# Wide products behind the four groups of a triangular inverse, and LayerNorm statistics from transposed blocks, in an encoder layer on one core

## The chip, the cores and the metric

The kernel runs on one core of a Trainium2 chip. The metric is the device time of one execution in microseconds; the median of 3 timed runs of the kernel before is 2743.46 us (2743.14 to 2744.37). The engines are called as the profile does: PE (TensorE, the products; PEld its weight loads), DVE (VectorE), ACT (ScalarE), POOL (GpSimd) and SP, which issues the DMAs.

## The reference: one encoder layer

Two groups of 512 tokens (a prompt and a sample), 1024 features, all in float32, shared weights:

```
x = LN(alpha*x + 0.5*SwiGLU_1(x))                      # d_ff 2816
h = x @ W_in                                           # MLA, RWKV-7 and gate columns
A = MLA(h_q, h_kv) @ P_mla ; B = RWKV7_bidir(h_rwkv) @ P_rwkv
x = LN(alpha*x + (sig(g_A)*A + sig(g_B)*B) @ W_o)      # LayerNorm 2
x = LN(alpha*x + CrossAttn(x, LN(mem)))                # LayerNorm 3
x = LN(alpha*x + 0.5*SwiGLU_2(x))
```

The RWKV-7 part has 8 heads of 64 and runs over the sequence in both directions. Per step the state S becomes `S*w + (S a) b^T + v k^T`, and the output is `S r`. LayerNorm is the plain one: mean and variance over the 1024 features of each token.

## The kernel before

**Products.** A float32 operand is held as two parts, hi and lo, each rounded for TensorE (fp32r); a product of two operands is hi·hi + hi·lo + lo·hi, three TensorE instructions of 128x512 for a block of 128 of the summed dimension. In names xh, xl (mh, ml; coh, col) are the parts of activations and whl both parts of a weight tile. `split` (L243-246) makes them: ACT casts the high part (L245), and the low part, the difference, is taken on an engine that the caller picks: POOL (L246) or DVE (all DVE operations show L179, a helper).

**Weights** of the middle of the program come through `Stream` (L113-150). A slot is a tile 128x1024, eight blocks: a DMA into wraw, the cast on ACT, the low part on `self.low`, at the moment `fetch` is called. `ahead` is how many slots are fetched before they are needed, 1 during the recurrence, where `low` is POOL.

**Stages**, by the trace of before: FFN 1 to about 715 us, projection and MLA to 1209, the recurrence to about 1750, mixing of the two branches and LayerNorm 2 to 1890, cross attention and LayerNorm 3 to 2065, FFN 2 and LayerNorm 4 to the end.

**The recurrence** (`Recurrence`) handles four pairs of heads in turn, h = 0 to 3. For each pair `front` builds the chunk matrices: 32 blocks (two directions, two groups, eight chunks of 64 tokens) of products ar,bk, masked into phi. `inverse` then inverts the unit triangular 64x64 matrices of these blocks: both 32x32 diagonal halves by forward substitution, all systems at once, on DVE (`for i in range(1, 31)`: a product tm, a step into dw, an add into dw), after which two DVE transposes give xt and ct; then the off-diagonal half by small TensorE products. These come in four groups of 32 products 32x32 per e (64 records each): two groups xt,phi, whose banks are copied to qt; two groups ct,qt, whose banks are copied into phi. Eight diagonal copies phi<-ct stand between. In these lines `k.in_order` fixes the order of the products among themselves. `chunks` runs the recurrence proper over the chunks, with products of 64x64.

TensorE would be idle for much of that, so `rec.beside` is a generator of wide products (the gates, the projections of the memory, the MLA output), and `Recurrence.fill(n)` takes n steps of it, a step being the three products of one k-block. The table `FILL` gives three numbers for each pair: steps asked for in the front, in the substitution (spread evenly over its 30 steps) and in the chunks. What is left at the last pair is done in `early_rows`.

**Norms 2 and 3** (`RowNorm`, L366-391) add up x and x² while the eight row blocks of 128 features come in: ACT squares, POOL (group 0) or DVE (group 1) adds x, DVE adds the squares; eight products with a column of 1/1024 (`mean`) then give mean and mean square per token. **Norms 1 and 4** (`BlockNorm`, L394) transpose the blocks on TensorE against an identity (cc), four 128x128 transposes into one bank, and take bn_stats of the bank on DVE (ln_b), then bn_aggr. PSUM banks carry tags: a has four banks, b and c two each (`Bank`).

**Order.** Each engine runs its instructions in an order that a scheduler fixes when the program is built; it moves work forward where it believes that there is room, so an instruction need not stand where the code has it.

Of the kernel before, what the change touches and what calls it, by code (L numbers as in the profile page):

```python
# [20 lines left out]
P = 128  # L21
T = 512
G = 2
# [37 lines left out]
FILL = ((72, 66, 30), (6, 50, 36), (8, 54, 36), (0, 38, 20))  # L61
# [302 lines left out]


class RowNorm(Norm):  # L366


    def add(self, n):
        nc, y = self.k.nc, self.y(n)  # L370
        if n == 0:
            self.s1, self.s2 = self.tile("ln_s1", 2), self.tile("ln_s2", 2)
        sq = self.tile("sq", 4) if n else self.s2
        nc.scalar.activation(out=sq, in_=y, func=AF.Square)
        if n:
            eng = nc.gpsimd if self.tags[0] == "c" else nc.vector
            eng.tensor_tensor(out=self.s1, in0=self.s1 if n > 1 else self.y(0), in1=y, op=ALU.add)
            nc.vector.tensor_tensor(out=self.s2, in0=self.s2, in1=sq, op=ALU.add)

    def stats(self):  # L380
        k, nc, sb = self.k, self.k.nc, self.sb
        st = Bank(k, self.tags[0])
        for o, t in enumerate((self.s1, self.s2)):
            for b in range(4):
                st.mm(st.t[:, 4 * o + b : 4 * o + b + 1], t[:, b * P : b * P + P], k.mean)
        m = sb.tile([P, 3, 4], F32, name="ln_m", tag="ln_m", bufs=2)
        mean, var, sq = m[:, 0], m[:, 1], m[:, 2]
        nc.vector.tensor_copy(m[:, 0:2], st.t[:, 0:8].rearrange("p (a b) -> p a b", b=4))
        nc.vector.scalar_tensor_tensor(out=sq, in0=mean, scalar=-1.0, in1=mean, op0=ALU.mult, op1=ALU.mult)
        nc.vector.scalar_tensor_tensor(out=var, in0=sq, scalar=LN_EPS / ALPHA**2, in1=var, op0=ALU.add, op1=ALU.add)  # L390
        Norm.spread([self], mean, var)
# [414 lines left out]
def kernel(  # L806
# [58 lines left out]
    k.mean = cp.tile([P, 1], F32, name="mean")  # L865
    nc.vector.memset(k.mean, 1.0 / D)
# [386 lines left out]
    with pool("rw") as sb:  # L1253
# [11 lines left out]

        rec.memory = memory_norm(k, sb, mem, d_mt)
# [45 lines left out]
    def norms_of(i):  # L1312
        return [RowNorm(k, sb, lambda n, g=g: x32[g][:, n], f"ln{i}_g", f"ln{i}_b", "cb"[g] * 2) for g in range(G)]

    for q in range(4):
        for g in range(G):
            nc.sync.dma_start(out=x32[g][:, 2 * q : 2 * q + 2], in_=d_x1[g][:, 2 * q : 2 * q + 2])
# [693 lines left out]
```

## Time and profile before

| | |
|---|---|
| median of 3 runs | 2743.46 us (2743.14 to 2744.37) |
| profiled execution, its own time | 2749.23 us |
| its span | 2747.4 us |
| granted clock of TensorE, mean | 0.971 |

The profile's page gives each engine's busy share, the span in 40 slices with the granted clock, the waits and the groups of instructions. Queries of the trace cut it into windows: length, busy time of each engine and the clock granted there. A length less PE's busy time is TensorE's idle time.

### The profile page before, as it was taken

What the parts mean: (1) busy time and instruction counts of PE and PEld (TensorE: products, weight loads), DVE (VectorE), ACT (ScalarE), POOL (GpSimd) and SP (SyncE); (2) the same over time, 40 slices, a digit from 0 to 9 for tenths busy, and PEclk for the clock granted to TensorE, in tenths of its full rate; (3) what the DMA queues carried; (4) which work ended last, traced back from release to release, by engine and by line L of the source; (5) the groups of instructions that cost most, each with busy time, mean ns of one, the idle gap of its engine ahead of it and who ended that gap; (6) DMA issues with size and microseconds to landing.
All of it is one profiled execution on the core that took longest, in us unless ns stands there. A gap on an engine that the chain in (4) does not pass through costs nothing.

```text
span 2747.4 us, 41481 instructions
## 1 busy us (share of the span) xinstructions
PE 2597.5 (95%) x15600; PEld 2074.1 (75%) x15600; DVE 2118.7 (77%) x3745; ACT 1090.2 (40%) x2004; POOL 699.2 (25%) x479
## 2 busy tenths in 40 slices
PE   8999999999999999997989888999999999999996
PEld 7888887787767777776677676777777888887784
DVE  7888887999466777758475768657788888887988
ACT  5344332222453555444443433224554433342222
POOL 0233332443200001133123331103031323232443
PEclk9999999999999999998999898999999999999998
DMA  4344337671244333343434353541102433347751
GB/s 173 123 154 161 146 135 297 237 264 64 92 171 157 114 97 112 115 139 136 132 110 128 119 179 116 166 157 46 47 31 81 165 143 139 141 173 266 275 200 65
DMA packets 164200, 396.08 MB, mean 144 GB/s; under 512 B 41056, under 2 KB 47456, under 8 KB 164000
## 3 DMA queue, kind: packets, MB, share of 16 engines
q1 hardware_dynamic: 164000, 393.43, 40.9%
q8 instruction: 124, 2.03, 0.3%
q14 instruction: 76, 0.62, 0.1%
HBM read 259.41 MB, written 133.96 MB: 143 GB/s over the span
## 4 chain that ended last, share of the span: by engine, by line
PE 54%; DVE 11%; issue 3%; ACT 3%; DMA 2%; POOL 1%; SPq 0%; POOLq 0%; ACTq 0%; DVEq 0%
PE ps L215 51%; PE ps L220 3%; DVE whl L179 1%; DVE dw L179 1%; DVE x L179 1%; DVE z L179 1%; DVE rs L179 1%; DVE phi L179 1%; DVE tm L179 1%; DVE ln_s L179 1%; DMA ld<-d_rw 1%; DVE wt L179 0%; ACT whl L245 0%; DMA d_q<-st 0%; POOL ln_z L357 0%
## 5 line engine op out<-in xcount | busy, mean ns | idle before, releaser
L215 PE MATMUL ps<-xo,whl 128*128 128x512 f32 x3792 | 899.3, 396 | 14.1 <-DVE z L179 8.5
L215 PE MATMUL ps<-xh,whl 128*128 128x512 f32 x2688 | 889.3, 402 | 15.7 <-ACT xh L245 11.4
L215 PEld LDWEIGHTS ps<-xo,whl 128*128 128x128 f32 x3792 | 712.9, 189 | 185.7 <-DVE z L179 6.7
L215 PEld LDWEIGHTS ps<-xh,whl 128*128 128x128 f32 x2688 | 508.1, 190 | 132.0 <-ACT xh L245 13.0
L215 PE MATMUL ps<-xl,whl 128*128 128x512 f32 x1344 | 536.5, 399 | 1.4 <-POOL xl L246 1.4
L179 DVE TENSOR_TENSOR whl<-wraw,whl 128x512 fp32r<-128x512 f32 (+4 forms) x269 | 280.4, 1052 | 53.2 <-ACT whl L245 52.7
L245 ACT CAST whl<-wraw 128x512 fp32r<-128x512 f32 (+4 forms) x314 | 219.7, 711 | 247.2 <-PE ps L215 226.4
L215 PEld LDWEIGHTS ps<-xl,whl 128*128 128x128 f32 x1344 | 255.9, 190 | 56.4 <-POOL xl L246 2.7
L712 POOL TENSOR_TENSOR s<-s,up 128x512 f32<-128x512 f32 x80 | 116.4, 1455 | 624.0 <-DVE up L179 399.7
L245 ACT CAST whl<-wt 128x512 fp32r<-128x512 f32 (+3 forms) x280 | 148.5, 555 | 272.5 <-PE ps L215 160.7
L179 DVE TENSOR_TENSOR whl<-wt,whl 128x512 fp32r<-128x512 f32 (+3 forms) x280 | 215.5, 791 | 11.5 <-ACT whl L245 11.4
L246 POOL TENSOR_TENSOR whl<-wraw,whl 128x1024 fp32r<-128x1024 f32 x45 | 109.4, 2433 | 385.8 <-ACT whl L245 353.3
L245 ACT CAST hop<-s 128x512 fp32r<-128x512 f32 x128 | 79.5, 621 | 246.1 <-POOL s L712 180.3
L179 DVE TENSOR_TENSOR hop<-s,hop 128x512 fp32r<-128x512 f32 x128 | 121.4, 949 | 58.3 <-ACT hop L245 50.7
L179 DVE SCALAR_TENSOR_TENSOR x<-ps,x 128x512 f32<-128x512 f32 x184 | 124.5, 683 | 53.6 <-PE ps L215 53.0
L179 DVE TENSOR_TENSOR wt<-wraw 128x512 f32<-128x512 f32 (+3 forms) x140 | 109.9, 785 | 1.0
L179 DVE TENSOR_TENSOR wt<-wraw,wt 128x512 f32<-128x512 f32 (+3 forms) x140 | 102.8, 734 | 4.6 <-DMA wraw<-in_wf_dram 2.6
L610 POOL TENSOR_TENSOR x<-x,s 128x512 f32<-128x512 f32 x48 | 70.6, 1476 | 129.4 <-DVE x L179 129.4
L246 POOL TENSOR_TENSOR xl<-x,xh 128x512 fp32r<-128x512 f32 x48 | 66.8, 1420 | 98.2 <-ACT xh L245 97.9
L179 DVE TENSOR_TENSOR p<-ps,p 128x512 f32<-128x512 f32 x120 | 82.2, 685 | 7.2 <-PE ps L215 4.0
L610 POOL TENSOR_TENSOR x<-x,z 128x512 f32<-128x512 f32 x48 | 71.2, 1485 | 52.8 <-DVE x L179 49.2
L215 PE MATMUL ps<-mh,whl 128*128 128x512 f32 x256 | 81.1, 397 | 1.3 <-ACT whl L245 1.3
(328 smaller groups left out, 3715.9 us busy)
## 6 DMA issues: line engine op xcount, KB each, us to landing
d_h<-hop SPq DMA_DIRECT2D x140, 512.0 KB, 2.6
xo<-d_h SPq DMA_DIRECT2D x140, 512.0 KB, 7.2
wraw<-in_wf_dram SPq DMA_DIRECT2D x95, 512.0 KB, 3.4
wraw<-in_wa_dram SPq DMA_DIRECT2D x57, 512.0 KB, 3.5
wraw<-in_wb_dram SPq DMA_DIRECT2D x32, 512.0 KB, 3.4
wraw<-in_wf_dram SPq DMA_DIRECT2D x36, 384.0 KB, 3.7
ld<-d_rw SPq DMA_DIRECT2D x24, 512.0 KB, 4.8
d_gate<-t SPq DMA_DIRECT2D x32, 256.0 KB, 2.3
```

Source lines behind the costliest of these rows:

```text
L179: inst = f(*args, **kw)
L215: self.last = order(k.tc, k.nc.tensor.matmul(out, a, b, start=start, stop=stop), self.last)
L220: self.last = order(self.k.tc, self.k.nc.tensor.transpose(out, a, ident), self.last)
L245: nc.scalar.copy(hi, src)
L246: (low or nc.vector).tensor_tensor(out=lo, in0=src, in1=hi.bitcast(F32), op=ALU.subtract)
L610: eng.tensor_tensor(out=y[r, c], in0=y[r, c], in1=u, op=ALU.add)
L712: nc.gpsimd.tensor_tensor(out=s[:, i], in0=s[:, i], in1=up[:, i], op=ALU.mult)
```

## The change

1. `FILL` asks for fewer steps in the substitution, and a new table `BESIDE` gives the steps that are placed directly behind each of the inverse's four groups: 2, 4, 2, 3 in the first three pairs, 0, 2, 0, 1 in the last. The sum of all steps is as before, since the generator is the same.
2. All four qt copies are on DVE (before, half of them were on ACT), and DVE's diagonal copies phi<-ct are ordered behind the last of them.
3. While the loop of the substitution is being emitted, `low` of the weight stream is DVE, and POOL again after it. Of the 45 low parts of 128x1024 that POOL had, 26 stay there; DVE has 74 in place of 55. Of the 19, six belong to the first pair, five each to the second and third, three to the fourth. In DVE's order 4, 2, 3 and 1 of them stand ahead of the four substitutions' first steps; 2, 3, 2 and 2 stand inside (the fourth pair's behind its last tm).
4. LayerNorms 2 and 3 are `BlockNorm`s: no squares on ACT, no running sums, no mean products; 32 transposes, eight bn_stats and four bn_aggr per norm and group. `add` is called after row blocks 3 and 7.
5. The weights of FFN 2 are set up before `out_rows(1)`, and three of its tiles are requested within it (`fw.ahead(1)`, after row blocks 7, 11 and 15 of its steps). The pool ow is opened earlier for that.

In the program's order, counted from a pair's last ar,bk product, the steps ahead of the first xt,phi product were 43, 47.3, 43.7 and 35.3, and are 32.7, 41.3, 33.7 and 37.3.

**TensorE around the inverse of the first pair, before.** The names xt,phi and ct,qt are the small products, xh and xl with whl the fill.

```order
L215 MATMUL ps<-xl_5605,whl 128x512
L215 MATMUL ps<-xh_5604,whl 128x512
L215 MATMUL ps<-xt,phi 32x32 x64
L215 MATMUL ps<-ct,qt 32x32 x25
L215 MATMUL ps<-xh_11155,whl 128x512
L215 MATMUL ps<-ct,qt 32x32 x6
L215 MATMUL ps<-xl_11156,whl 128x512
L215 MATMUL ps<-xh_11155,whl 128x512
L215 MATMUL ps<-ct,qt 32x32 x18
L215 MATMUL ps<-xh_11155,whl 128x512
L215 MATMUL ps<-ct,qt 32x32 x12
```

**The same place in the changed kernel.**

```order
L217 MATMUL ps<-xl_5603,whl 128x512
L217 MATMUL ps<-xh_5602,whl 128x512
L217 MATMUL ps<-xt,phi 32x32 x32
L217 MATMUL ps<-xh_5602,whl 128x512
L217 MATMUL ps<-xl_5603,whl 128x512
L217 MATMUL ps<-xh_5602,whl 128x512 x2
L217 MATMUL ps<-xl_5603,whl 128x512
L217 MATMUL ps<-xh_5602,whl 128x512
L217 MATMUL ps<-xt,phi 32x32 x32
L217 MATMUL ps<-xh_5600,whl 128x512
L217 MATMUL ps<-xl_5601,whl 128x512
L217 MATMUL ps<-xh_5600,whl 128x512 x2
```

The first 64 rows of xt,phi were one run and are two of 32, with two steps between; four steps follow the second, two the first run of ct,qt and three the second.

**DVE at the end of the substitution and in the copies of the first pair, before** (tm, dw: the substitution; qt<-ps the copies out of the xt,phi banks).

```order
L179 SCALAR_TENSOR_TENSOR dw<-dw,lw 128x29
L179 TENSOR_TENSOR dw<-dw,tm 128x29
L179 SCALAR_TENSOR_TENSOR dw<-dw,lw 128x30
L179 STREAM_TRANSPOSE xt<-dw 128x32x32
L179 STREAM_TRANSPOSE ct<-dw 128x32x32
L179 COPY phi<-ct 32x16x32 x4
L179 COPY qt<-ps 32x512 x2
L179 COPY phi<-ps 32x16x32
L179 TENSOR_TENSOR xl_11156<-t,xh_11155 128x512
L179 COPY phi<-ps 32x16x32
```

**The same place in the changed kernel**, and above it the low part inside the chain, behind the step 22:

```order
L181 TENSOR_TENSOR tm<-lw,dw 128x176
L181 SCALAR_TENSOR_TENSOR dw<-dw,lw 128x22
L181 TENSOR_TENSOR whl<-wraw,whl 128x1024
L181 TENSOR_TENSOR dw<-dw,tm 128x8x22
L181 TENSOR_TENSOR tm<-lw,dw 128x161
L181 SCALAR_TENSOR_TENSOR dw<-dw,lw 128x23
```

```order
L181 MEMSET dw 128x32
L181 SCALAR_TENSOR_TENSOR dw<-dw,lw 128x29
L181 TENSOR_TENSOR dw<-dw,tm 128x29
L181 TENSOR_SCALAR mem<-mem,bag 128x1024
L181 SCALAR_TENSOR_TENSOR dw<-dw,lw 128x30
L181 STREAM_TRANSPOSE xt<-dw 128x32x32
L181 STREAM_TRANSPOSE ct<-dw 128x32x32
L181 COPY qt<-ps 32x512 x4
L181 COPY phi<-ct 32x16x32 x4
L181 COPY phi<-ps 32x16x32 x2
L181 COPY uv<-ps 64x2x2x64
```

A weight's low part stands between a product tm and its add, the four qt copies come ahead of the four diagonal copies, and an operation on mem that had stood elsewhere is inside the chain.

**TensorE at LayerNorm 3 of the first group, before** (xpt,xv: attention; coh, col: the output projection; mean,ln_s: the sums of the norm).

```order
L215 MATMUL ps<-coh_18194,whl 128x512
L215 MATMUL ps<-col_18195,whl 128x512
L215 MATMUL ps<-xpt,xv 128x256 x5
L215 MATMUL ps<-mean,ln_s_18283 128x1 x4
L215 MATMUL ps<-coh_18194,whl 128x512 x2
L215 MATMUL ps<-mean,ln_s_18284 128x1 x4
L215 MATMUL ps<-col_18195,whl 128x512
L215 MATMUL ps<-coh_18194,whl 128x512 x2
L215 MATMUL ps<-col_18195,whl 128x512
```

**The same place in the changed kernel** (cc,x: transposes, four per bank).

```order
L217 MATMUL ps<-xpt,xv 128x256
L222 MATMUL ps<-cc,x_16870 128x128 x4
L217 MATMUL ps<-xpt,xv 128x256 x5
L222 MATMUL ps<-cc,x_16870 128x128 x12
L217 MATMUL ps<-coh_17755,whl 128x512
L217 MATMUL ps<-col_17756,whl 128x512
L217 MATMUL ps<-coh_17755,whl 128x512 x2
L217 MATMUL ps<-col_17756,whl 128x512
L217 MATMUL ps<-coh_17755,whl 128x512
```

The eight products with a column of this norm (two times four) become two halves of 16 transposes; one half is shown, with twelve of its transposes in one run.

The diff, without the class that it removes (`RowNorm`, told above):

```diff
--- before.py
+++ after.py
@@ -58,7 +58,9 @@
 PAUSE = 8
 A_FILL = A_END - 16
 
-FILL = ((72, 66, 30), (6, 50, 36), (8, 54, 36), (0, 38, 20))
+
+FILL = ((72, 46, 34), (8, 44, 30), (10, 44, 34), (0, 40, 16))
+BESIDE = ((2, 4, 2, 3),) * 3 + ((0, 2, 0, 1),)
 STREAM_B = (
     tiles_of("w_ck", range(4), 8)
     + [("w_cv", k, n) for k in range(8) for n in range(4)]
...
@@ -862,8 +836,6 @@
     nc.vector.memset(k.ones, 1.0)
     k.half = cp.tile([P, 1], F32, name="half")
     nc.vector.memset(k.half, 0.5)
-    k.mean = cp.tile([P, 1], F32, name="mean")
-    nc.vector.memset(k.mean, 1.0 / D)
     vc = cp.tile([P, NVEC], F32, name="vc")
     nc.sync.dma_start(out=vc, in_=vec)
 
@@ -1263,6 +1235,7 @@
                 ys.append(Acts(xpools[0], "x", 4, HP, "y"))
                 rows(ys[g], [d_y[h][g] for h in range(HP - 1)])
 
+        rec.weights = st
         rec.memory = memory_norm(k, sb, mem, d_mt)
         for h, beside in enumerate(FILL):
             rec.front(h, beside[0])
@@ -1309,21 +1282,23 @@
     y32 = keep.tile([P, G, KT, T], F32, name="x32")
     x32 = [y32[:, g] for g in range(G)]
 
-    def norms_of(i):
-        return [RowNorm(k, sb, lambda n, g=g: x32[g][:, n], f"ln{i}_g", f"ln{i}_b", "cb"[g] * 2) for g in range(G)]
+    def norms_of(i, *tags):
+        return [BlockNorm(k, sb, lambda n, g=g: x32[g][:, n], f"ln{i}_g", f"ln{i}_b", tags[g]) for g in range(G)]
 
     for q in range(4):
         for g in range(G):
             nc.sync.dma_start(out=x32[g][:, 2 * q : 2 * q + 2], in_=d_x1[g][:, 2 * q : 2 * q + 2])
+    ow = ctx.enter_context(pool("ow", "right"))
     wb_pool = cross.enter_context(pool("wb", "right"))
     st.use((wp, 3, 2), (wb_pool, 2, 0), (wp, 3, 2), (wb_pool, 2, 0), (wp, 3, 2))
 
     def sum_row(norm, g, n, b, f):
         y = x32[g][:, n]
         nc.vector.scalar_tensor_tensor(out=y, in0=b.t, scalar=f, in1=y, op0=ALU.mult, op1=ALU.add)
-        norm.add(n)
-
-    norms = norms_of(2)
+        if n % 4 == 3:
+            norm.add(n // 4)
+
+    norms = norms_of(2, ("c", "b"), ("c", "c"))
     w = []
 
     def mix_rows(g, ns):
@@ -1340,11 +1315,11 @@
         for g in range(G):
             mix_rows(g, range(n0, n0 + 4))
             if (n0, g) == (4, 0):
-                norms[0].stats()
+                BlockNorm.stats(norms[:1], False)
     x2 = [None, None]
     for g in range(G):
         if g:
-            norms[g].stats()
+            BlockNorm.stats(norms[1:], False)
         x2[g] = (acts if g else others)(KT, "x")
         norms[g].apply(x2[g])
 
@@ -1430,22 +1405,23 @@
     kvs[1] = memory_of(1)
     xo[1] = acts(4, "co")
     w = [st.blocks(4) for _ in range(KT)]
-    norms = norms_of(3)
+    norms = norms_of(3, ("a", "b"), ("c", "c"))
     both(attend(1), out_rows(0))
-    norms[0].stats()
-    for _ in out_rows(1):
-        pass
+    BlockNorm.stats(norms[:1], False)
+    fw = FfnWeights(k, wf2, [(wp, 3)] * 3 + [(ow, 1)], [(wp, 2)] * 2 + [(ow, 1)], ow)
+    for i, _ in enumerate(out_rows(1)):
+        if i % 4 == 3 and i > 4:
+            fw.ahead(1)
     x3 = [None, None]
     for g in range(G):
         if g:
-            norms[g].stats()
+            BlockNorm.stats(norms[1:], False)
         x3[g] = acts(KT, "x")
         norms[g].apply(x3[g])
 
 
     cross.close()
-    ow, of = ctx.enter_context(pool("ow", "right")), ctx.enter_context(pool("of"))
-    fw = FfnWeights(k, wf2, [(wp, 3)] * 3 + [(ow, 1)], [(wp, 2)] * 2 + [(ow, 1)], ow)
+    of = ctx.enter_context(pool("of"))
     ln = []
 
     def sums2():
@@ -1703,6 +1679,8 @@
         dw = t4("dw")
         nc.scalar.copy(dw, lw)
         lm, dm = lw.rearrange("p (i k) -> p i k", k=32), dw.rearrange("p (i k) -> p i k", k=32)
+
+        self.weights.low = nc.vector
         for i in range(1, 31):
             if i < 30:
                 tm = self.sb.tile([P, 256], F32, name="tm", tag="tm", bufs=2)
@@ -1720,6 +1698,7 @@
             if i < 30:
                 o = dm[:, i + 2 : 32, 0:i]
                 nc.vector.tensor_tensor(out=o, in0=o, in1=t, op=ALU.add)
+        self.weights.low = nc.gpsimd
         nc.vector.memset(dw[:, 0:1024:33], 1.0)
         xt, ct = t4("xt"), t4("ct")
         nc.vector.transpose(out=tj(xt), in_=dw.rearrange("p (t s) -> p s t", s=32))
@@ -1729,23 +1708,30 @@
         ra, rb = ([slice(64 * e + o, 64 * e + o + 32) for e in range(2)] for o in (0, 32))
 
         k.in_order, k.pe_last = True, None
-        for j0, tag in ((0, "c"), (16, "b")):
+        for n, (j0, tag) in enumerate(((0, "c"), (16, "b"))):
             ps = [self.bank(tag) for _ in range(2)]
             for j in range(16):
                 for e in range(2):
                     ps[e].mm(ps[e].t[rb[e], j * 32 : j * 32 + 32], phi[ra[e], e, j0 + j, 32:64], xt[ra[e], j0 + j])
-            for e, cp in ((0, nc.scalar.copy), (1, nc.vector.tensor_copy)):
-                cp(qt[rb[e], j0 : j0 + 16], ps[e].t[rb[e]].rearrange("p (j s) -> p j s", s=32))
+            for e in range(2):
+                last = nc.vector.tensor_copy(
+                    qt[rb[e], j0 : j0 + 16], ps[e].t[rb[e]].rearrange("p (j s) -> p j s", s=32))
+            self.fill(BESIDE[h][n])
         for j in (0, 16):
             for q in range(4):
-                (nc.scalar.copy if q % 2 else nc.vector.tensor_copy)(diag(q, j), ct[32 * q : 32 * q + 32, j : j + 16])
-        for j0, tag in ((0, "c"), (16, "b")):
+                to, src = diag(q, j), ct[32 * q : 32 * q + 32, j : j + 16]
+                if q % 2:
+                    nc.scalar.copy(to, src)
+                else:
+                    order(k.tc, nc.vector.tensor_copy(to, src), last)
+        for n, (j0, tag) in enumerate(((0, "c"), (16, "b"))):
             ps = [self.bank(tag) for _ in range(2)]
             for j in range(16):
                 for e in range(2):
                     ps[e].mm(ps[e].t[ra[e], j * 32 : j * 32 + 32], qt[rb[e], j0 + j], ct[rb[e], j0 + j])
             for e, cp in ((0, nc.scalar.copy), (1, nc.vector.tensor_copy)):
                 cp(phi[ra[e], e, j0 : j0 + 16, 32:64], ps[e].t[ra[e]].rearrange("p (j s) -> p j s", s=32))
+            self.fill(BESIDE[h][2 + n])
         k.in_order = False
 
     def chunks(self, h, beside, early_rows):
```

More of the change, by code (lines that the diff above doesn't have):

```diff
@@ L363, in applying @@
             yield
[L366 to L391, printed above, removed]
 class BlockNorm(Norm):
```

## The prediction

> **What bounds the kernel now.** I read the page's busy shares and granted clock first, then the list of waits of TensorE, then windows around the places that the change touches.
>
> ```profile
> span 2747.4 us, 41481 instructions
> PE 2597.5 (95%) x15600; PEld 2074.1 (75%) x15600; DVE 2118.7 (77%) x3745; ACT 1090.2 (40%) x2004; POOL 699.2 (25%) x479
> PEclk9999999999999999998999898999999999999998
> ```
>
> TensorE (PE) is busy for 95% of the span, so a change can win only its idle 150 us and the slices where the clock row shows less than 9. The waits of TensorE in the recurrence, from 1209 to 1750 us (time, times, longest), begin with:
>
> ```profile
> PE ps L215 <- DVE xt L179: 25.1, 4, 8.5
> PE ps L215 <- ACT qt L1738: 9.5, 3, 4.3
> ```
>
> Once in each of the four head pairs TensorE runs out of wide products before VectorE (DVE) has solved the triangular systems and transposed the result (xt); three times it then waits until ScalarE (ACT) has copied qt. The next view cuts each pair into three stretches: from the first step of the substitution to the first product of xt; the small products of the inverse; the wide products after them, for as long as the clock stays down. Columns: stretch, length, busy time (and records) of PE, weight loads, DVE, ACT, POOL, granted clock, DMA share, GB/s. The last row is an undisturbed stretch of FFN 1.
>
> ```profile
> 1262.20:1291.10 28.90, 21.58 (x96) 17.54 (x95) 28.83 (x92) 6.36 (x8) 10.35 (x4) 0.92 0.40 137
> 1291.10:1306.50 15.40, 11.73 (x262) 8.98 (x262) 6.88 (x10) 7.97 (x14) 4.83 (x3) 0.50 0.47 147
> 1306.50:1313.60 7.10, 6.57 (x84) 5.41 (x84) 2.42 (x5) 3.32 (x7) 2.55 (x2) 0.50 0.83 282
> 1400.80:1429.80 29.00, 25.92 (x115) 21.16 (x114) 28.88 (x91) 6.42 (x9) 9.86 (x4) 1.00 0.33 109
> 1429.80:1442.20 12.40, 7.39 (x258) 7.13 (x260) 5.98 (x9) 7.80 (x12) 4.64 (x2) 0.50 0.31 94
> 1442.20:1446.80 4.60, 4.14 (x37) 3.45 (x38) 2.10 (x3) 1.69 (x3) 1.62 (x1) 0.50 1.16 262
> 1537.80:1567.30 29.50, 23.40 (x104) 19.04 (x102) 29.37 (x91) 5.69 (x8) 11.00 (x5) 0.98 0.34 117
> 1567.30:1577.80 10.50, 7.53 (x261) 7.29 (x263) 6.04 (x9) 5.71 (x9) 2.35 (x1) 0.50 0.17 51
> 1577.80:1583.30 5.50, 5.04 (x42) 3.69 (x42) 2.95 (x4) 1.69 (x3) 1.39 (x1) 0.50 0.74 164
> 1667.20:1694.60 27.40, 18.39 (x79) 14.09 (x77) 27.38 (x99) 2.10 (x2) 2.44 (x1) 0.90 0.51 168
> 1694.60:1702.60 8.00, 7.12 (x257) 6.88 (x257) 6.00 (x9) 4.80 (x9) 0.00 (x0) 0.50 0.63 181
> 1702.60:1709.60 7.00, 6.54 (x83) 5.39 (x83) 5.01 (x11) 1.75 (x3) 4.26 (x2) 0.50 0.35 78
> 50.00:100.00 50.00, 50.00 (x220) 40.98 (x219) 37.52 (x56) 21.10 (x36) 8.18 (x6) 1.00 0.28 96
> ```
>
> DVE is full in every first stretch (28.83 of 28.90 us): the substitution is the bound there, and TensorE's idle time is length less busy, 7.3, 3.1, 6.1 and 9.0, together 25.5 us. Among the small products it idles 3.7, 5.0, 3.0 and 0.9, together 12.6 us. The clock is 0.50 through them and for 24.2 us after them (7.1 + 4.6 + 5.5 + 7.0). A wide product at full clock takes 50.00/220 = 0.227 us, and one fill step, three of them, 0.68 us.
>
> **The substitution.** The chain's steps are short, except where a low part runs on POOL:
>
> ```profile
> 1259.73 2.59 DVE L179 TENSOR_SCALAR mem<-mem,bag 128x1024 f32<-128x1024 f32 x1
> ...
> 1263.43 0.26 DVE L179 TENSOR_TENSOR tm<-lw,dw 128x104 f32<-128x104 f32 x1
> 1263.76 2.50 POOL L246 TENSOR_TENSOR whl<-wraw,whl 128x1024 fp32r<-128x1024 f32 x1 [1.99 <-ACT whl L245]
> 1263.92 2.48 DVE L179 TENSOR_TENSOR tm<-lw,dw 128x125 f32<-128x125 f32 x1
> 1284.36 0.33 DVE L179 TENSOR_TENSOR tm<-lw,dw 128x176 f32<-128x176 f32 x1
> L179 DVE TENSOR_TENSOR whl<-wraw,whl 128x1024 fp32r<-128x1024 f32 x5 | 6.1, 1221 | 1.9 <-ACT whl L245 1.9
> ```
>
> The DVE step that begins under a POOL low part ends with it: 2.48 us, where its neighbours of 104 and 176 columns take 0.26 and 0.33. So each low part costs the chain about 2.2 us; four, four, four and one of them start inside the four substitutions: 8.8, 8.8, 8.8, 2.2 us. On DVE itself a low part takes 1.22 us, and the new order puts 2, 3, 2 and 2 inside the chains: 2.4, 3.7, 2.4, 2.4. Each chain is shorter by 6.4, 5.1, 6.4 and -0.2 us. (In the first pair the operation on mem, 2.59 us, moves from directly ahead of the chain to near its end: for xt's time that is nothing.)
>
> That is no gain for TensorE by itself, since the change also takes fill from ahead of xt. Counted in the order of TensorE's instructions from the pair's last ar,bk product, 43, 47.3, 43.7 and 35.3 steps become 32.7, 41.3, 33.7 and 37.3: at 0.68 us 7.0, 4.1, 6.8 and -1.4 us less work. Idle before xt becomes 7.3+7.0-6.4 = 7.9, 3.1+4.1-5.1 = 2.1, 6.1+6.8-6.4 = 6.5 and 9.0-1.4+0.2 = 7.8: 24.3 us, hardly less than 25.5. Part of it will now show as waits for DVE's whl in mid-substitution: in the first pair the low part stands behind step 22, where its products are due some 3 us earlier. Queued behind such a low part is the rest of the chain, and so xt; its 1.22 us are in the sum. The moved products go to where TensorE idles now.
>
> **Behind the groups.** What ScalarE does while TensorE waits for qt, in the second pair:
>
> ```profile
> 1431.46 2.50 ACT L1741 COPY phi<-ct 32x512 f32<-32x512 f32 x4 [13.96 <-DVE ct L179]
> 1437.15 1.05 ACT L1738 COPY qt<-ps 32x512 f32<-32x512 f32 x2
> 1437.78 3.62 PE L215 MATMUL ps<-ct,qt 32*32 32x32 f32 x128 [4.34 <-ACT qt L1738]
> L179 DVE COPY qt<-ps 32x512 f32<-32x512 f32 x8 | 5.3, 693 | 1.4 <-PE ps L215 1.4
> ```
>
> The qt copies stand behind four diagonal copies, two gate activations and two casts. On DVE a copy takes 0.69 us, two 1.4, ahead of the diagonals; the 2 to 4 fill steps behind each group are 1.4 to 2.7 us of wide products at full clock. So the copies are covered but for about 0.5 us a pair, 2.0 in all. Without that cover TensorE would wait for them 0.7 to 1.4 us behind each of the four groups, 3 to 6 us a pair. Idle around the inverse goes from 25.5 + 12.6 = 38.1 to 24.3 + 2.0 = 26.3: **-11.8 us**.
>
> **The clock** has two ends. If the fill steps between the groups bring it back, up to half of the 24.2 us is won, -12.1. If it stays at half through all groups, the 36 steps moved there take 0.68 us more each, +24.5, and nothing is won. After the second pair's groups it came back within 4.6 us of mixed products; so I let the first 2 steps and half of the next 4 run slow in three pairs (12 x 0.68 = +8.2) and win three chunk starts at half of 17.2 us (-8.6). The fourth pair, whose groups get 0, 2, 0, 1 steps, stays as it is. Taken: **-0.5**, between -10 and +12 as what I think possible.
>
> The Trainium skill (TensorE: Matmul & The Clock Gate, HAM oscillation — how this bites in real kernels) says that the clock falls after TensorE has idled for longer than about 3.4 us. In the second pair it fell after an idle stretch of 3.08 us, so the trace disagrees a little; by that rule gaps of 2 us, as I expect there, would keep it up, which is the rival on the clock below.
>
> **VectorE in the front.** Ten low parts stand on DVE ahead of their chains (4, 2, 3, 1), 10 x 1.22 = 12.2 us if all of it delays xt; where one replaces a POOL low part that stalled DVE, it wins 1. Between -2 and +12 I take a quarter, since the front also waits for DMAs and products: **+3**. Taking fill from the chunks (36 to 30, 36 to 34, 20 to 16 steps, 30 to 34 in the first) is the same work at another place, +0..4, in the range only.
>
> **LayerNorms 2 and 3.** What goes and what comes, per norm, by these rows (transposes and statistics as they stand in norms 1 and 4):
>
> ```profile
> 1896.16 1.05 PE L215 MATMUL ps<-mean,ln_s 128*128 128x1 f32 x8 [0.48 <-DVE ln_s L179]
> 1897.63 0.95 PE L215 MATMUL ps<-mean,ln_s 128*128 128x1 f32 x8
> 654.71 1.03 PE L220 MATMUL ps<-cc,x 128*128 128x128 f32 x8
> 2700.86 0.66 PE L220 MATMUL ps<-cc,x 128*128 128x128 f32 x4 [1.36 <-DVE ln_b L179]
> L179 DVE BATCH_NORM_STATS2 ln_b<-ps x32: 673/685/700, 656.4 to 2721.6; 128x6 f32<-128x512 f32 x32
>   PE ps L220: 2.3, 3
> L179 DVE TENSOR_TENSOR ln_s<-ln_s,sq 128x512 f32<-128x512 f32 x22 | 21.7, 987 | 4.3 <-ACT sq L374 4.0
> ```
>
> PE loses 2.0 us and gains 32 transposes, 4 x 1.03 = 4.1 with modelled ends: +1.8 to +2.1 each, +7 for four norms. DVE loses some seven adds of 0.99 and gets eight statistics of 0.69; that and ScalarE's squares lie beside PE, at no price. Three of the four norms use tag c with its two banks, so the third and fourth burst of a half can wait for a statistic, 12 times in all: in norms 1 and 4 (the row "PE ps L220" of who waited for ln_b) 2.3 us in 3 waits, the longest 1.36. I take +1.5, of 0 to 12 x 1.36 = 16.3. Two rows on the place of norm 3:
>
> ```profile
> 2008.00:2020.00 12.00, 11.45 (x58) 9.35 (x57) 6.98 (x23) 2.01 (x4) 1.29 (x1) 0.86 0.01 2
> 2040.00:2072.00 32.00, 27.47 (x126) 21.39 (x126) 31.66 (x51) 20.02 (x31) 17.54 (x11) 1.00 0.16 51
> ```
>
> The mean products stood where the clock dipped to 0.86 over 12 us: its loss, 1.7, goes. Of the 4.5 us that PE idles on the way into FFN 2, with DVE full, three of FFN 2's first weight tiles now come earlier, their DVE work with them: -2.5, of 0 to -4.5. One us of the transposes falls into waits that are there anyway. Norms and FFN 2: 7 + 1.5 - 1.7 - 2.5 - 1 = **+3.3**, from -3 to +20.
>
> The same skill page (Part 4: PE-mode transpose) says that transposes don't count as work for the clock. In this trace they stand between products and the clock is full:
>
> ```profile
> 654.70:671.10 16.40, 16.40 (x96) 13.49 (x95) 15.43 (x24) 2.62 (x3) 0.61 (x1) 1.00 0.30 97
> ```
>
> By the rule eight bursts could each halve one stretch of 3.4 us, an estimate of +13.7 us; the trace speaks against it.
>
> **Sum.** -11.8 - 0.5 + 3 + 3.3 = -6.0 us. The profiled execution took 2749.23 (span 2747.4 and 1.8 around it), so 2743.2; it lies 5.8 above the median, 2743.46, and the same difference gives **2737 us**.
>
> **Rivals.** (1) The clock comes back: with gaps of 2 us in place of 3 to 5 the second pair never falls, the first and third recover in their first fill, and the norms cost half. -11.8 - 10 + 1 (front) + 1 (norms) = about -20: 2724 us. For it speaks the 4.6 us recovery, against it that 24 of 25 us before xt stay idle. Chance 0.2. (2) VectorE's own low parts and the transposes eat the gain: front +6, norms +7, clock -0.5: about 0, 2744 us. DVE being full before xt speaks for it. Chance 0.2. (3) Slower: the bank waits. The 12 waits for a statistic meet a DVE that is 99% busy at norm 3 (31.66 of 32.00). At w each, the sum is -9.3 + 7 - 1.7 - 2.5 + 12w = 12w - 6.5; it turns at w = 0.54 us and is slower by 0.2% from 1.0. With w = 1.36, +9.8: 2753 us. Against it: 2.3 us in three waits at norms 1 and 4. Chance 0.13. (4) The low parts of the substitution are not on TensorE's path and xt is as late as before: idle before xt becomes 25.5 + 16.5 (the moved fill) = 42.0, the groups still win 10.6, and the whole is +5.9 - 0.5 + 3 + 3.3 = +11.7: 2755 us. The step of 2.48 us in a full DVE speaks against it: 0.04.
>
> **How the numbers follow.** My own case has 0.43. Of it 0.42 lies more than 0.2% (5.5 us, about what a measurement here tells from no change) below the median, with the clock's 0.2 and 0.01 of rival 2 that is faster 0.63; 0.01 of mine and 0.18 of rival 2 lie within 0.2%, 0.19 + 0.01 of rival 3 is same 0.20; the rest, 0.01 of rival 2, 0.12 of rival 3 and 0.04 of rival 4, is slower 0.17. The range takes in the clock and most of the bank waits: 2717 to 2751.
>
> **What would show it.** TensorE's waits for xt still near 24 us, some of it under DVE whl; waits for ACT's qt gone; no step over 1 us in the substitutions but the low parts; the clock back to 1.00 before the first chunk product in three pairs; 256 transposes cc,x in place of 128, with waits for ln_b below 4 us. I am wrong if xt comes no earlier, if the groups stay at 0.50 to their end, or if ln_b waits pass 7 us.

## The result

The changed kernel takes 2730.09 us (median of 5 runs, 2727.45 to 2731.69), before 2743.46 (5 runs, 2741.42 to 2748.01): a ratio of 0.9938, 95% interval 0.9922 to 0.9953. That is 13.4 us won by the medians (17 by the ratio, by which the experiments below are counted) where 6.5 were forecast; the time lies inside the range. Its profiled execution took 2731.69 us. The page after:

```profile
span 2729.9 us, 41526 instructions
PE 2592.1 (95%) x15664; PEld 2074.1 (76%) x15664; DVE 2100.2 (77%) x3769; ACT 1069.4 (39%) x1964; POOL 632.2 (23%) x446
PEclk9999999999989999998999989999999999999998
```

The spans differ by 17.5 us. Of these 3.8 had been won before the recurrence began (it starts at 1212.2 us before and at 1208.4 after), where the program differs only by an unused constant of 4 bytes that the change drops. Over the other profiles of this study it starts between 1203 and 1210 us, so that part is mostly scatter between executions. The waits of TensorE from 1209 to 1750 us in the changed kernel (time, times, longest):

```profile
PE ps L217 <- DVE xt L181: 21.9, 4, 8.0
PE ps L217 <- ACT gs L1766: 11.7, 30, 1.0
...
PE ps L217 <- DVE whl L181: 5.0, 2, 3.6
PE ps L222 <- ACT mt L1528: 2.6, 5, 1.4
PE ps L217 <- ACT yo L1876: 2.3, 2, 2.0
```

The 9.5 us for ACT's qt are gone, as forecast. But xt and whl together are 26.9 us where xt alone was 25.1, and gs (9.1 before), mt and yo have grown. The windows of the four pairs, the substitution up to the first xt product and then the groups up to the first chunk product:

```profile
1257.40:1282.50 25.10, 16.93 (x67) 13.23 (x66) 25.07 (x96) 4.99 (x6) 2.35 (x1) 0.93 0.37 115
1282.50:1299.20 16.70, 16.68 (x288) 13.16 (x288) 9.51 (x11) 7.34 (x13) 2.36 (x1) 0.69 0.33 87
1397.80:1423.60 25.80, 22.27 (x99) 18.14 (x98) 25.72 (x95) 6.76 (x9) 2.37 (x1) 0.98 0.45 143
1423.60:1438.90 15.30, 15.30 (x289) 12.11 (x289) 9.11 (x12) 6.93 (x11) 6.32 (x3) 0.81 0.35 94
1532.20:1556.60 24.40, 17.08 (x73) 13.28 (x73) 24.33 (x93) 4.70 (x6) 2.34 (x1) 0.98 0.36 107
1556.60:1572.00 15.40, 15.39 (x291) 12.21 (x291) 8.49 (x12) 6.18 (x9) 6.68 (x3) 0.81 0.35 95
1659.30:1685.80 26.50, 18.54 (x84) 15.07 (x83) 26.47 (x101) 2.11 (x2) 0.00 (x0) 0.93 0.59 192
1685.80:1695.20 9.40, 9.40 (x265) 7.88 (x265) 8.01 (x12) 3.77 (x7) 1.00 (x1) 0.66 0.55 161
```

TensorE's idle time at the groups, 12.6 us before, is nothing now (0.03). Ahead of xt it is 8.2 + 3.5 + 7.3 + 8.0 = 27.0 us, a little more than the 25.5 before: what the chains won, the missing fill lost. The whole recurrence, first before and then after:

```profile
1212.20:1797.50 585.30, 513.59 (x6079) 415.02 (x6078) 393.42 (x885) 225.44 (x408) 146.03 (x94) 0.91 0.44 140
```

```profile
1208.40:1789.70 581.30, 516.86 (x6080) 413.80 (x6078) 392.84 (x912) 223.04 (x401) 97.66 (x75) 0.93 0.45 141
...
1313.30:1320.10 6.80, 5.24 (x27) 3.30 (x26) 4.00 (x7) 4.77 (x11) 0.28 (x1) 0.50 0.66 181
1443.00:1449.80 6.80, 5.75 (x54) 4.61 (x56) 5.89 (x17) 0.38 (x1) 0.08 (x1) 0.50 0.35 102
1603.40:1620.50 17.10, 15.08 (x183) 13.52 (x179) 7.21 (x14) 6.98 (x13) 4.66 (x4) 0.50 0.67 229
```

It is only 4.0 us shorter: idle 71.7 to 64.4, and 3.3 us more busy for the same number of products. The last three rows show places in the chunks of the first, second and third pair where the clock was at 0.50; in the third TensorE had no wide product from 1599.2 to 1618.3 us, and the clock stayed down for 17.1.

How far one profile can be trusted here is seen in two runs below, `tail_only` and `norm_only`, whose recurrence is that of before:

```profile
1206.90:1799.90 593.00, 516.94 (x6080) 417.92 (x6078) 395.85 (x885) 225.73 (x409) 144.79 (x94) 0.91 0.45 138
1206.30:1792.30 586.00, 513.70 (x6080) 414.13 (x6078) 394.26 (x885) 225.53 (x408) 144.92 (x94) 0.91 0.45 140
```

The same recurrence takes 585.3 to 593.0 us, with TensorE busy for 513.6 to 516.9. So neither the 4.0 us nor the 3.3 are clear of scatter by this one pair of profiles.

The rest was won behind the recurrence. From the recurrence's end to the start of FFN 2's main part (its first product with xo) the changed kernel takes 295.8 us in place of 301.5; the main part, 2631 records of products, takes 4.0 us less with nothing changed in it. Before (the mixing's output product with norm 2; attention and norm 3; the way into FFN 2; the main part) and after:

```profile
1798.70:1892.90 94.20, 93.34 (x409) 75.06 (x410) 51.94 (x78) 28.92 (x41) 19.95 (x14) 1.00 0.25 93
1892.90:2037.30 144.40, 136.31 (x689) 110.09 (x689) 113.76 (x292) 76.29 (x178) 26.52 (x21) 0.96 0.14 44
2037.30:2099.00 61.70, 57.17 (x253) 45.03 (x252) 54.81 (x84) 35.16 (x56) 18.84 (x12) 1.00 0.19 69
2099.00:2718.30 619.30, 611.41 (x2631) 490.34 (x2630) 532.14 (x731) 205.33 (x384) 204.13 (x136) 1.00 0.47 173
```

```profile
1790.70:1887.50 96.80, 96.55 (x442) 77.87 (x443) 45.33 (x74) 21.30 (x28) 12.20 (x8) 1.00 0.30 107
1887.50:2028.70 141.20, 134.72 (x722) 110.96 (x721) 115.35 (x300) 71.58 (x168) 19.12 (x15) 0.99 0.16 50
2028.70:2085.50 56.80, 56.15 (x253) 45.10 (x251) 44.59 (x76) 29.20 (x47) 14.46 (x10) 1.00 0.09 38
2085.50:2700.80 615.30, 606.95 (x2631) 490.28 (x2631) 531.68 (x731) 205.15 (x384) 204.76 (x136) 1.00 0.48 174
  PE ps L222: 2.9, 4
```

(The last line after is who waited for ln_b.) Norm 2's stretch is 2.6 us longer, the two behind it are 3.2 and 4.9 shorter. So the direction was right and the win twice as large as forecast, in part by luck: the recurrence gave less than forecast in this profile, the norms, forecast to cost 3.3, won, and 4.0 us came from FFN 2's main part, which no term named.

### The profile page after: what moved, and what is told of

The parts are those of the page before. It is cut to its first block, busy times and chain, and to the rows that moved or that the text cites. A ratio compares the mean times of both kernels' runs of the same rounds, so it can differ in the third digit from the quotient of the medians.

```text
span 2729.9 us, 41526 instructions
## 1 busy us (share of the span) xinstructions
PE 2592.1 (95%) x15664; PEld 2074.1 (76%) x15664; DVE 2100.2 (77%) x3769; ACT 1069.4 (39%) x1964; POOL 632.2 (23%) x446
## 4 chain that ended last, share of the span: by engine, by line
PE 53%; DVE 12%; ACT 3%; DMA 2%; issue 2%; POOL 1%; SPq 0%; POOLq 0%; DVEq 0%; ACTq 0%
PE ps L217 50%; PE ps L222 3%; DVE whl L181 2%; DVE dw L181 2%; DVE z L181 1%; DVE tm L181 1%; DVE phi L181 1%; DVE x L181 1%; DVE rs L181 1%; ACT whl L247 1%; DMA wraw<-in_wb_dram 0%; DVE wt L181 0%; POOL ln_z L359 0%; DVE gm L181 0%; ACT x L360 0%
## 5 line engine op out<-in xcount | busy, mean ns | idle before, releaser
L217 PEld LDWEIGHTS ps<-xh,whl 128*128 128x128 f32 x2688 | 509.3, 191 | 128.2 <-ACT xh L247 12.1
L181 DVE TENSOR_TENSOR whl<-wraw,whl 128x512 fp32r<-128x512 f32 (+4 forms) x288 | 300.5, 1053 | 72.2 <-ACT whl L247 71.7
L248 POOL TENSOR_TENSOR whl<-wraw,whl 128x1024 fp32r<-128x1024 f32 x26 | 63.3, 2436 | 384.6 <-ACT whl L247 278.8
```

Of the source, the lines that this page charges most:

```text
L181: inst = f(*args, **kw)
L217: self.last = order(k.tc, k.nc.tensor.matmul(out, a, b, start=start, stop=stop), self.last)
L248: (low or nc.vector).tensor_tensor(out=lo, in0=src, in1=hi.bitcast(F32), op=ALU.subtract)
```

## The experiments

Each kernel was timed in turns with the kernel before; ratios are to it, with 95% intervals. 0.1% is 2.7 us.

**The recurrence alone and the tail alone.** `rec_only` has RowNorm and FFN 2's weights as before:

```diff
-def norms_of(i, *tags): return [BlockNorm(...)]
+def norms_of(i): return [RowNorm(...)]
-for i, _ in enumerate(out_rows(1)): ... fw.ahead(1)
+for _ in out_rows(1): pass          # FfnWeights built behind norm 3
```

> The recurrence's part of the change alone (fill behind the groups, qt copies and low parts on VectorE), with LayerNorms 2 and 3 and FFN 2's weights as before. The prediction's sum: -11.8 - 0.5 + 3 = -9.3 us against before. The rival from the two profiles (from the start of the recurrence to the end of the mixing the changed kernel gains 4.0 us): -4 us. TensorE's waits for xt and whl: 24 us by the first, 27 by the second, with the lost part in waits for gs, mt and yo inside the chunks.

Measured: 0.9978 (0.9965 to 0.9991), -6.0 us, between -2.5 and -9.6. Both numbers lie inside; its profile has 585.2 us for the recurrence, no less than before (that execution took 2746.9 us, its median is 2739.5). The waits of 26 us are there as in the changed kernel (xt 21.2, whl 5.0).

`tail_only` is the other half: old `FILL`, no `BESIDE`, old qt copies, low parts on POOL, with the new norms and weights.

> LayerNorms 2 and 3 with transposed blocks and FFN 2's three early weight tiles, on the recurrence as before. The prediction's sum: +3.3 us. The rival from the two profiles: -6 us (norm 2 +2.6, attention and norm 3 -3.2, the way into FFN 2 -4.9, rounded to what runs repeat), with TensorE's idle time between norm 3 and FFN 2's first down product below 1.5 us in place of 4.5.

Measured: 0.9974 (0.9964 to 0.9985), -7.1 us. The term +3.3 is refuted. TensorE's idle time on the way into FFN 2 is 0.7 us in its profile (4.5 before), as the rival said.

`norm_only` is `tail_only` with FFN 2's weights as before. (The weights alone, with RowNorm, were not run.)

> LayerNorms 2 and 3 with transposed blocks alone, FFN 2's weights requested as before. If the norms' own price is as predicted (7 us of transposes, waits and clock about even), +4 to +6 us, and then the early weights win 5 or more. If the way into FFN 2 is won by the lighter norm (VectorE and ScalarE have less to do there), -2 to -4 us, and the early weights win 1 to 3 on top.

Measured: 0.9971 (0.9959 to 0.9983), -8.0 us. So by time the early weights can't be told from nothing here. In the profiles the way into FFN 2 takes 61.7 us before, 58.6 with the norms, 56.9 with the weights too. From the recurrence's end to FFN 2's main part it is 301.5 us before and in `rec_only`, 296.8 with the norms, 295.9 with the weights too. That is some 5 us of the 8.0, and most of the rest lies in FFN 2's main part (619.3 before, 615.3 in `norm_only`, 617.2 in `tail_only`), which is not the norms' work; the run with four bytes below returns to it.

**The low parts alone.** `low_only` has only `self.weights.low = nc.vector` in the substitution.

> Only the low parts of the weights go to VectorE during the substitution; fill table, qt copies, norms and FFN 2 as before. By the prediction's sum the chains are 17.7 us shorter and all fill still lies ahead of xt, so TensorE's idle time ahead of xt falls from 25.5 to about 8 us and the whole by 15 (17.7 less 3 in the fronts). The rival: TensorE gets what the chain wins only where it idled (3.1 us in the second pair), and the low parts come too late for their products, so waits for whl take 5 us or more: -6 us.

Measured: 0.9919 (0.9904 to 0.9934), -22 us: more than the 17 of the whole change by the same measure, though the two intervals overlap. Its waits:

```profile
PE ps L216 <- DVE xt L180: 13.9, 4, 8.5
...
PE ps L216 <- ACT qt L1743: 5.3, 2, 3.9
```

The fill still lies ahead of xt, and so 11.2 us of the 25.1 are gone, where the sum had 17.7; no wait for whl is on the list. A further 4.2 us went from the waits for qt, although ACT's copies are as before. The recurrence is 17 us shorter in its profile. So this one setting wins 22 us, and the rest of the recurrence's part gives 16 of them back (`rec_only`, 6.0).

**Which part gives it back.** `low_tail` is the changed kernel without the fill behind the groups and with the old qt copies; `low_qt_tail` has the new qt copies too, and so differs from the changed kernel in the table alone:

```diff
-FILL = ((72, 46, 34), (8, 44, 30), (10, 44, 34), (0, 40, 16))
-BESIDE = ((2, 4, 2, 3),) * 3 + ((0, 2, 0, 1),)
+FILL = ((72, 66, 30), (6, 50, 36), (8, 54, 36), (0, 38, 20))
-            self.fill(BESIDE[h][n])
-            self.fill(BESIDE[h][2 + n])
```

> The changed kernel with the old fill table, nothing behind the groups, and the old qt copies: only the low parts on VectorE, the norms and the early weights are left of the change. If the parts add up (0.81% for the low parts alone, 0.26% for norms and weights), the ratio to before is 0.989 to 0.990, some 14 us below the changed kernel, and the moved fill is what costs the changed kernel its gain. If the fill behind the groups does win what the prediction gave it (10.6 us of waits around the small products), it is slower than the changed kernel: ratio over 0.994.

> The changed kernel with the old fill table alone: low parts and qt copies on VectorE, norms, early weights. In the run with the low parts alone TensorE waited 5.3 us for ScalarE's qt in two places. If these waits go with the order of the copies, it is 4 to 5 us faster than the same kernel with the old copies (ratio 0.987 to 0.988). If they only turn into waits for the diagonal copies or for VectorE's qt, the two are equal.

Measured: 0.9878 (0.9860 to 0.9897) and 0.9859 (0.9840 to 0.9877), 2714.7 and 2707.5 us with 2747.0 for the kernel before. The fill behind the groups costs the changed kernel 0.79% (0.9938 less 0.9859), 22 us. The intervals of `low_tail` and `low_qt_tail` overlap: the qt copies may win 5 us, but the runs don't show it. The profiles say the same of the fill: the recurrence takes 585.3 to 593.0 us in the three with the recurrence of before, 581.3 to 585.2 in three with the changed one (`after_pad` below is the third) and 557.8 to 563.1 in three with the old table and the new copies (`pad64` and `no_early_weights` below are the others). The windows of `low_qt_tail`, cut as above:

```profile
1253.50:1278.90 25.40, 22.00 (x99) 17.92 (x99) 25.37 (x98) 8.37 (x10) 1.63 (x1) 1.00 0.50 146
1278.90:1290.60 11.70, 11.14 (x262) 8.52 (x262) 9.00 (x12) 5.40 (x10) 3.42 (x3) 0.52 0.81 266
1384.40:1410.60 26.20, 26.20 (x117) 21.46 (x115) 26.12 (x95) 8.25 (x10) 2.42 (x1) 1.00 0.45 133
1410.60:1416.60 6.00, 4.66 (x257) 4.27 (x256) 5.08 (x8) 5.18 (x9) 1.23 (x1) 0.94 0.46 142
1516.50:1541.30 24.80, 23.84 (x104) 19.08 (x102) 24.77 (x95) 6.82 (x8) 0.82 (x1) 1.00 0.45 137
1541.30:1548.50 7.20, 5.81 (x256) 5.35 (x256) 6.88 (x11) 3.61 (x6) 1.55 (x1) 0.80 0.59 151
1634.80:1661.20 26.40, 17.72 (x79) 14.34 (x78) 26.37 (x100) 2.11 (x2) 0.00 (x0) 0.88 0.51 172
1661.20:1668.80 7.60, 7.00 (x256) 6.89 (x256) 6.82 (x11) 3.64 (x7) 0.00 (x0) 0.50 0.62 179
```

Ahead of xt TensorE idles 3.4 + 0 + 1.0 + 8.7 = 13.1 us, and at the groups 0.6 + 1.3 + 1.4 + 0.6 = 3.9 us, with no more fill there than six wide products in the first pair. So fill behind the groups had 3.9 us left to win, and costs 13.9 (27.0 - 13.1) ahead of xt. In the second pair TensorE never stops before xt; the clock is 0.94 through the small products, which take 6.0 us where they took 12.4. It falls to 0.50 right behind them, from 1415.9 to 1426.2 us.

**Is it the place taken from, or the place put to?** `beside_from_chunks` keeps the steps behind the groups, but takes them from the chunks:

```diff
-FILL = ((72, 46, 34), (8, 44, 30), (10, 44, 34), (0, 40, 16))
+FILL = ((72, 66, 19), (6, 50, 25), (8, 54, 25), (0, 38, 17))
```

> Low parts and qt copies on VectorE, norms and early weights, the same steps behind the four groups as in the changed kernel, but taken from the chunks behind them (30, 36, 36, 20 steps become 19, 25, 25, 17) and not from ahead of xt, which keeps its 43, 47, 44 and 35. If the loss of the changed kernel lies ahead of xt (TensorE idles there when its fill is taken away), this kernel is within 4 us of the one with the old table (2707.5). If it lies at the groups themselves (wide products at half clock, 36 x 0.68 us at most), it keeps most of the loss: 2718 to 2730.

Measured: 0.9861 (0.9845 to 0.9876), 2709.4 us: the loss lay ahead of xt. The group stretches of its second and third pair, and what the chunks now wait for:

```profile
1411.10:1424.00 12.90, 12.90 (x291) 10.24 (x291) 9.77 (x12) 7.72 (x11) 2.55 (x1) 1.00 0.38 105
1541.90:1554.80 12.90, 12.85 (x289) 10.27 (x289) 8.09 (x12) 5.63 (x8) 6.13 (x4) 1.00 0.45 112
```

```profile
PE ps L217 <- DVE uv L181: 9.6, 6, 4.6
...
PE ps L217 <- DVE sn L181: 5.8, 6, 1.9
```

Here the fill keeps the clock at 1.00 through the groups, but the chunks, which had waited 3.7 us for uv in `low_qt_tail`, wait 9.6. Over the recurrence, idle time rises by 6.7 us (51.4 to 58.0) and busy time falls by 9.3 (511.7 to 502.5); the times are the same within the intervals.

`rebal` is `low_qt_tail` with six steps each taken from the second and third pair's chunks (36 to 30) and twelve given to the last substitution (38 to 50).

> Low parts and qt copies on VectorE, norms, early weights, and a table of fill that takes six steps each from the chunks of the second and third pair (36 to 30) and gives them to the last pair's substitution (38 to 50), where TensorE still waited 8.5 us for xt. If these steps are only moved into idle time, 12 x 0.68 = 8 us faster than the same kernel with the old table. If the chunks need them as cover for their own waits (gs, uv), 0 to 3 us faster or slower.

Measured: 0.9876 (0.9857 to 0.9895): no gain. The waits for xt fall from 13.1 to 9.3 us. Its profile has the recurrence at 564.1 us against 563.1: what xt no longer waits is lost elsewhere. That fits the chunks' need of their cover, but no run shows which wait took it.

**The low parts in the changed kernel.** `no_low` is the changed kernel without the two lines that set `low`.

> The changed kernel with POOL's low parts in the substitution: fill behind the groups, qt copies, norms, early weights. By the prediction's sum the chains are 17.7 us longer and nothing else changes, so 2748 us, about the time of before plus 4, and TensorE's waits for xt and whl rise from 27 to some 42 us. The rival, by which VectorE's low parts win only what they win where fill covers them: 2738 us or less.

Measured: 0.9983 (0.9973 to 0.9993), 4.7 us below before. Its stretches ahead of xt:

```profile
1255.40:1282.10 26.70, 14.73 (x67) 11.88 (x67) 26.63 (x92) 4.68 (x6) 7.67 (x3) 0.87 0.35 109
1397.70:1427.30 29.60, 22.11 (x98) 17.99 (x97) 29.52 (x91) 6.51 (x8) 10.80 (x5) 0.91 0.40 125
1534.90:1562.40 27.50, 16.52 (x73) 13.33 (x72) 27.43 (x91) 4.61 (x6) 8.37 (x4) 0.87 0.34 106
1662.50:1690.30 27.80, 19.57 (x85) 15.20 (x83) 27.73 (x99) 2.12 (x3) 2.79 (x2) 0.90 0.59 195
```

Idle: 12.0 + 7.5 + 11.0 + 8.2 = 38.7 us, 11.7 more than with VectorE's low parts (42 were expected). By time the low parts are worth 0.45%, 12 us here. The time, 2742.7 us, lies between the two that were expected, 2748 and 2738: the low parts win less beside the new table than with the old one (12 against 22 us), as the rival had it, but more than it allowed.

**The early weights.** `no_early_weights` is `low_qt_tail` with FFN 2's weights as before.

> Low parts and qt copies on VectorE, old table of fill, transposed norms, and FFN 2's weights requested as before, behind the norm. The prediction gave the early weights 2.5 us of the way into FFN 2. If they win that, 2710; if the lighter norm wins all of it, within 1.5 us of the kernel with the early weights (2707.5).

Measured: 0.9865 (0.9848 to 0.9883), 2708.4 us. The way into FFN 2 takes 59.1 us against 56.8, so 2.3 us are won there. By time the two are equal, although its FFN 2 main part is 2.1 us longer too (617.2 and 615.1): its profile has the recurrence, which is the same program, 5.3 us shorter (557.8), so differences of this size are within the scatter.

**Four bytes.** `after_pad` is the changed kernel with the unused constant back:

```diff
     nc.vector.memset(k.half, 0.5)
+    k.mean = cp.tile([P, 1], F32, name="mean")
+    nc.vector.memset(k.mean, 1.0 / D)
```

> The changed kernel with one thing put back that nothing uses any more: the constant mean, one column of 4 bytes per partition, which lies ahead of nearly all other tiles. In the profiles without it the 1896 products of FFN 2's main part take 615.3 us (617.1 in one), with it 619.3, and those of FFN 1 1 us less. If that comes from where the tiles lie in the memory, FFN 2's part takes 619 us again and the whole is 4 to 5 us slower than the changed kernel. If it comes from the norms or the early weights, it stays at 615.3 and the time is that of the changed kernel.

Measured: FFN 2's main part is back at 619.3 us, with nothing else changed in it:

```profile
2087.40:2706.70 619.30, 612.64 (x2631) 492.17 (x2630) 530.71 (x730) 205.13 (x384) 204.23 (x136) 1.00 0.48 173
```

The four kernels with the constant (before, `rec_only`, `low_only`, `after_pad`) all have 619.3; the nine without any have 615.1 to 618.2, six of them at most 615.7. By time `after_pad` stands at 0.9949 (0.9932 to 0.9966), which does not separate it from the changed kernel's 0.9938.

`pad64` is `low_qt_tail` with 64 bytes in that place.

> The fastest kernel so far (low parts and qt copies on VectorE, old table of fill, norms, early weights) with an unused constant of 64 bytes per partition where the one of 4 bytes lay. If the speed of the products in the FFNs depends on where tiles lie within some 64 bytes, FFN 2's main part takes 615 us as without a constant. If any move of the tiles changes it, another value than 615.1 and 619.3.

Measured: 0.9857 (0.9841 to 0.9872), 2707.1 us, FFN 2's main part 618.3 us. That is neither 615.1 nor 619.3, but `rebal`, without a constant, has 618.2 too. So the expectation of 64 bytes as a period isn't met, and the runs don't say by what rule the place acts; why `tail_only`, `no_early_weights` and `rebal` lie at 617 to 618 stays open.

## Why the prediction was right, and where it was wrong

**What bounds the kernel:** right. The waits for xt and for the groups were where time could be had, and POOL's low parts inside the chain cost about what the rows of 2.5 us said.

**The chains:** forecast 17.7 us shorter, measured 28.9 + 28.9 + 29.4 + 27.4 before against 25.1 + 25.8 + 24.4 + 26.5, 12.8 us. The step that failed took every POOL low part out of the chain. One each is left in the first three (POOL x1 in the windows after), and it still stretches what runs beside it. VectorE in the second pair and in the first:

```profile
1416.30 1.24 DVE L181 TENSOR_TENSOR whl<-wraw,whl 128x1024 fp32r<-128x1024 f32 x1
1418.22 2.42 DVE L181 SCALAR_TENSOR_TENSOR dw<-dw,lw 128x28 f32<-128x28 f32 x1
```

```profile
1277.32 2.86 DVE L181 TENSOR_SCALAR mem<-mem,bag 128x1024 f32<-128x1024 f32 x1
```

In the second pair that is a step of 2.42 us, in the third one of 2.22 (at 1552.2 us), and there the chain is 2.0 and 1.4 us longer than forecast. In the first pair the stretched operation is the one on mem. It was stretched before as well (2.59 us), but then it stood ahead of the window, so the 2.6 us that are missing in this pair are no loss for xt, as the prediction said. The fourth chain came out 1.1 us better than forecast.

**Idle time around the inverse:** forecast 38.1 to 26.3, measured 38.1 to 27.0. That the sum was right is partly luck, and it hid the mistake. It set the fill that leaves xt (16.5 us of work) against the waits at the groups (10.6 us won) without pricing the change with the old table. By its own numbers that would have had 25.5 - 17.7 = 8 us idle ahead of xt; at the groups, without the fill, it saw waits of 3 to 6 us a pair. `low_qt_tail`, without it, has 13.1 ahead of xt and 0.6 to 1.4 a pair at the groups, 3.9 in all. That price was the term that failed. The waits at the groups were credited to the fill; most had gone with the low parts (8.2 us are left in the profile of `low_tail`) and the order of the copies.

**The clock:** forecast -0.5. It did come back before the first chunk product, in all four pairs (0.69 to 0.81 over the groups of three, and 0.66 in the last). TensorE's busy time rose by 3.3 us, which the scatter between equal recurrences can make as well, so the term is neither borne out nor refuted. What it left out is that the clock falls again in the chunks, for 6.8 us in the first two pairs and 17.1 in the third. That this comes from the fill taken from the chunks, which the prediction called "the same work at another place", is not shown. `rec_only`, with the same table, has 3.4 us at 0.50 in the third pair's chunks, and `beside_from_chunks`, which takes more from them, has the clock at 0.95 over the recurrence, against 0.93 in the changed kernel and 0.91 before.

**Fronts:** +3 was forecast; idle time outside the inverse rose by 3.8 us (71.7 to 64.4 is 7.3, and the inverse accounts for 11.1). The waits that grew are gs, mt and yo, which lie in the chunks and not in the fronts, so the size fits by chance and the place doesn't. Together -11.1 + 3.8 + 3.3 = -4.0 us for the recurrence by the profile; by time -6.0 with an interval that takes in the forecast -9.3.

**Norms and FFN 2:** forecast +3.3, by the profile -5.7, by time -7.1 (with what lies in FFN 2's main part). The transposes cost less than 7 us: from start to start 128 take 12.1 us and the 64 records of mean products 6.9, so 5.2. The waits for ln_b went from 2.3 to 2.9 us over the whole program, so the +1.5 and the rival of bank waits were too high. The clock in attention and norm 3 went from 0.96 to 0.99 over some 140 us, about twice the 1.7 us that one dip was given: by the traces three stretches of 3.4 us at 0.50 before and in `rec_only`, one in the changed kernel, `norm_only` and `tail_only`. The step that failed is "beside PE, at no price". From shortly before the recurrence's end to FFN 2's main part VectorE is busy 15 us less (230.0 to 214.9), and TensorE idles 8.3 us where it idled 14.7. Where VectorE had been full (54.81 of 61.70 us over the whole way into FFN 2, all of it in its middle), its work was not free. ScalarE has less to do there too (144.8 to 126.6 us), and no run separates the two. The early weights' 2.5 us were sized about right: 2.3 in one pair of profiles, 1.7 in the other.

The Trainium skill (TensorE: Matmul & The Clock Gate, Part 4: PE-mode transpose) would have made the transposes cost clock. In the stretch of norm 2 with 50 of its 64 transposes the clock is 1.00, so the trace disagrees again. The Trainium skill's rule on gaps over 3.4 us (the same page, HAM oscillation — how this bites in real kernels) does not cover what these runs show. In `low_qt_tail`, in the pair in which TensorE never stopped ahead of xt, the clock fell at 1415.9 us with no wait longer than 0.5 us among the small products before it. In `beside_from_chunks` waits of 1.1 and 1.0 us ahead of xt left it at 1.00. Whether a gap of 2 us would do was not seen, since the second pair of the changed kernel kept 3.5 us.

**FFN 2's main part**, 4.0 us, was in no term. Without it the changed kernel would have lain near 2734, still 2.9 below the forecast.

**The rivals:** the clock (2724) came back at the groups and fell again in the chunks; VectorE's own low parts did show as waits for whl, 5.0 us, but within the sum; bank waits didn't come; the low parts were on the path, as `no_low` shows.

## What to carry to other kernels

When a change does two things, price each with the other left out: here one setting wins 22 us, and the table beside it takes most of that back, while the sum over both looked like a gain. Cover work is worth what it covers after the other edits, not before them; here the waits behind the groups had shrunk from 12.6 to 3.9 us before any fill was put there. `low_qt_tail`, which keeps the old table, takes 2707.5 us, 1.4% below before and 0.8% below the changed kernel; no run of this study is clearly faster.

## What the runs showed of the hardware that was not expected

An unused constant of 4 bytes per partition ahead of the other tiles goes with some 4 us of the 615 that FFN 2's main part takes, through products that start 1.6 ns further apart on the mean (235.6 ns before, 234.0 in the changed kernel). By which rule is open. And the clock can stay at 0.50 for 17 us with TensorE 88% busy (15.08 of 17.10), while it does only products of 64x64 and 128x64 and few wide ones.
